# A QKV projection on one core: three leading row pairs multiplied without sums in place of two, and an identity tile of another size

## The chip, the cores and the metric

The kernel runs on one core of a Trainium2 chip. Its time is device microseconds for one execution; the time of a kernel is the median of its runs.

## The reference

```python
def reference(x, w_qkv):                      # x (16, 512, 768), w_qkv (768, 2304), float32
    qkv = np.matmul(x, w_qkv)
    hidden = x.shape[-1]
    q = qkv[..., :hidden]
    k = qkv[..., hidden:2*hidden]
    v = qkv[..., 2*hidden:]
    return np.stack([q, k, v], axis=0).astype(np.float32)
```

One product of 8192 rows by 768 by 2304, whose columns are written to three outputs. Both inputs are standard normal numbers.

## The kernel before

The 8192 rows are taken in 32 pairs of row blocks, 128 rows each. The 2304 columns are two "quads" of 1024 columns (q = 0 at the left, q = 1 at the right), each of two halves of 512, and a middle remainder of 256 columns. The 768 contraction rows are six slices of 128 (KT = 6), in two halves of three (KH = 3). So for a pair and a quad the product is one of 2 by 2 block matrices, and it is computed in one of two ways.

*Unsummed* (`block`, L378): plain bf16 matmuls, eight block products, that is 24 matmuls of 128x512 for a pair and a quad, 48 for a pair. `b1[q]` holds the bf16 weights of a quad's first column half, `bt` those of the second.

*Summed* (`do` and `product`, L193 to L246): seven products in place of eight, by Winograd's form of Strassen's method. Sums of x's blocks (`sums_x`, L177, on GpSimd) and of the weights' blocks (`sum_w`, L98, on VectorE) are multiplied, and the results are added up in PSUM and in the output tile. A pair costs 42 matmuls of 128x512. Products 1 and 2 use bf16 (`xb` and `b1`); the other five use f32r (float32r, 4 bytes an element): the stationary side is a slice of `s`, the moving side one of the four weight sums `t1` to `t4` or `b22`. The sums for quad 0 lie in `t_0`, in the w pool; those for quad 1 in two tiles `t_1`, which take over the buffers of the staged weights in pool tq.

In both ways the remainder is 12 bf16 matmuls of 128x256 for a pair (`rem`, L262).

Matmuls need x with its contraction axis on the partitions. For most pairs `load_x` brings x in 32-row groups with four DMAs, `transpose` (L124) turns 32x32 blocks on VectorE, and `round_x` (L175) casts to bf16 on GpSimd. The first three pairs are loaded as plain rows (`load_rows`) and turned by TensorE against an identity: pairs 0 and 1 after a cast to bf16 (`cast_rows`, `turn_bf16`, L158), pair 2 in fp32 (`turn_fp32`, L169), since its sums need fp32. `copy_two` (L139, L140) splits each of the casts and copies between VectorE and ScalarE.

The order of all work is written out by hand; each engine takes its instructions in the order of the program. At the start: warm-up matmuls on zeros, pairs 0 and 1 turned, block (0,0) [quad 0, first half] of pairs 0 and 1, their remainders, pair 2 turned, then blocks (0,1), (1,0) and (1,1) of pairs 0 and 1, with ScalarE casting the weights of the block that follows. Meanwhile VectorE makes the weight sums and GpSimd casts `bt0`'s second half (L376), `b22[0]` (L429) and `b22[1]` (L439) and makes pair 2's `xb` and sums. Pairs 2 to 31 are summed: `two` interleaves quad 0 (a) and quad 1 (b) of a pair in the order a1 b1 a2 a6 b2 b6 a5 a7 b5 b7 a4 remainder b4 a3 b3. Its `early`, after b1, transposes and sums the next pair and starts the load of the one after. The last pair has its own order (`last`).

SP issues nearly all DMAs, in order: three row loads and all the weights at the start, then stores and the loads of x. Of the output tiles `o` (two row blocks by 1024 columns) there are five buffers, of `xin` three, of `xb` four, of `xf` and `s` two. [...]

The w pool holds, in order of allocation, w_rem, b1 (2), b22 (2), t_0, zero, tiny and the identities; the pools that follow it in memory (tq, bt, o, st, xin, xf, xb, s) start where it ends.

Of the kernel before, what the change touches and what calls it, by code (L numbers as in the profile page):

```python
# [10 lines left out]
def kernel(  # L11
# [20 lines left out]
    nc = tc.nc  # L32
    P = 128
# [5 lines left out]
    KT = K // P  # L39
    KH = KT // 2  # L40
    KC = K // 4
    NP = M // (2 * P)
    CB = 512
# [3 lines left out]
    fp32 = mybir.dt.float32  # L47
# [51 lines left out]
    def sum_w(q, n):  # L99
        t1, t2, t3, t4 = ts[q]  # L100
        o, in0, in1 = {
            1: (t1, stage[q, 0, 1], stage[q, 0, 0]),
            2: (t2, stage[q, 1, 1], t1),
            3: (t3, stage[q, 1, 1], stage[q, 0, 1]),
            4: (t4, stage[q, 1, 0], t2),
        }[n]
        nc.vector.tensor_tensor(o, in0, in1, op=sub)
# [5 lines left out]
    def load_x(p, other):  # L113
        xin[p] = xin_pool.tile([P, 2 * P // G, KC], fp32, name="xin")
        t = xin[p]
        rows = x_flat[p * 2 * P:(p + 1) * 2 * P, :].rearrange("(g b) k -> b g k", b=G)
        for n in range(2):
            for h in range(2):
                i = 2 * h + n
                (nc.sync, other)[h].dma_start(t[i * G:(i + 1) * G], rows[:, :, i * KC:(i + 1) * KC])  # L120
# [13 lines left out]
        rows = x_flat[p * 2 * P:(p + 1) * 2 * P, :]  # L134
        nc.sync.dma_start(xin[p][:], rows.rearrange("(r m) k -> m r k", m=P))

    def copy_two(dst, src):

        nc.vector.tensor_copy(out=dst[0], in_=src[0])  # L139
        nc.scalar.activation(dst[1], src[1], ident)  # L140

    xc = {}

    def cast_rows(p):
        src = xin.pop(p)
        xc[p] = s_pool.tile([P, 2, K], bf16, name="xc", tag="s")
        for r in range(2):
            halves = (slice(0, K // 2), slice(K // 2, K))
            copy_two([xc[p][:, r, n] for n in halves], [src[:, r, n] for n in halves])

    def turn_bf16(p):
        c = xc.pop(p)
        xb[p] = xb_pool.tile([P, KT, 2 * P], bf16, name="xb")
        for r in range(2):
            cols = c[:, r, :].rearrange("m (p j) -> m j p", j=KT)
            ps = ps_pool.tile([P, KT, P], bf16, name="ps")
            for j in range(KT):
                nc.tensor.transpose(ps[:, j, :], cols[:, j, :], eye_b[:])  # L158
            ks = (slice(0, KH), slice(KH, KT))
            copy_two([xb[p][:, n, r * P:(r + 1) * P] for n in ks], [ps[:, n, :] for n in ks])  # L160

    def turn_fp32(p):
        src = xin.pop(p)
        xf[p] = xf_pool.tile([P, KT, 2 * P], fp32, name="xf")
        for r in range(2):
            cols = src[:, r, :].rearrange("m (p j) -> m j p", j=KT)
            ps = [ps_pool.tile([P, KH, P], fp32, name="ps") for _ in range(2)]
            for j in range(KT):
                nc.tensor.transpose(ps[j // KH][:, j % KH, :], cols[:, j, :], eye[:])  # L169
            ks = (slice(0, KH), slice(KH, KT))  # L170
            copy_two([xf[p][:, n, r * P:(r + 1) * P] for n in ks], [t[:] for t in ps])

    def round_x(p):
        xb[p] = xb_pool.tile([P, KT, 2 * P], bf16, name="xb")
        nc.gpsimd.tensor_copy(out=xb[p][:], in_=xf[p][:])  # L175

    def sums_x(p):  # L177
        t = xf.pop(p)
        a11, a12 = t[:, :KH, :P], t[:, KH:, :P]
        a21, a22 = t[:, :KH, P:], t[:, KH:, P:]  # L180
        s = s_pool.tile([P, 5, KH, P], f32r, name="s")
        g = nc.gpsimd
        g.tensor_tensor(s[:, 1], a21, a22, op=add)  # L183
        g.tensor_tensor(s[:, 2], s[:, 1], a11, op=sub)  # L184
        g.tensor_tensor(s[:, 3], a11, a21, op=sub)  # L185
        g.tensor_copy(out=s[:, 0], in_=a22)
        g.tensor_tensor(s[:, 4], a12, s[:, 2], op=sub)  # L187
        sr[p] = s
# [5 lines left out]
    def quad(p, q):  # L194
        u = Quad()
        u.p, u.q = p, q
        u.o = o_pool.tile([P, 2, 2 * CB], fp32, name="o", tag="o")
        u.x = u.y = u.z = None
        return u
# [17 lines left out]
    def bank():  # L217
        return ps_pool.tile([P, CB], fp32, name="ps")
# [32 lines left out]
    def store_quad(u):  # L251
        if u.q == 0:
            nc.sync.dma_start(rows_of(0, u.p, 0, H), u.o[:, :, :H])
            nc.sync.dma_start(rows_of(1, u.p, 0, 2 * CB - H), u.o[:, :, H:])
        else:
            part = 2 * H - Q_OFF[1]
            nc.sync.dma_start(rows_of(1, u.p, H - part, H), u.o[:, :, :part])
            nc.sync.dma_start(rows_of(2, u.p, 0, H), u.o[:, :, part:])
# [8 lines left out]
    def rem(p):  # L267
        ps = ps_pool.tile([P, 2, REM], fp32, name="ps")
        for r in range(2):
            rem_row(p, r, ps[:, r, :])  # L270
        o = or_pool.tile([P, 2, REM], fp32, name="orem")
        nc.scalar.activation(o[:], ps[:], ident)  # L272
        nc.sync.dma_start(rows_of(1, p, R_OFF - H, R_OFF - H + REM), o[:])
# [67 lines left out]
        rem_stored(1)  # L341


    zero = w_pool.tile([P, CB], bf16, name="zero")
    nc.vector.memset(zero[:], 0.0)
    load_rows(0)
    tiny = w_pool.tile([P, 1], fp32, name="tiny")
    nc.scalar.activation(tiny[:], zero[:, :1], ident)
    eye = w_pool.tile([P, P], fp32, name="eye")
    make_identity(nc, eye)  # L350
    eye_b = w_pool.tile([P, P], bf16, name="eye_b")
    make_identity(nc, eye_b)
    load_rows(1)
    load_blocks(0, 0, 1)
    st_rem = o_pool.tile([P, KT, REM], fp32, name="str", tag="o")
    load_w(st_rem[:], 0, KT, R_OFF, REM)
    load_rows(2)
    load_blocks(0, 1)
    o0 = [quad(p, 0) for p in range(2)]
    load_blocks(1, 0)  # L360
    load_blocks(1, 1)
    o1 = [quad(p, 1) for p in range(2)]

    def busy(n):

        ps = bank()
        for _ in range(n):
            nc.tensor.matmul(ps[:], zero[:, :P], zero[:], start=True, stop=True)

    def cast(q, h, c, w, eng):  # L370

        dst = w[:, h * KH:(h + 1) * KH, :]
        if eng is nc.scalar:
            eng.activation(dst, stage[q, h, c], ident)  # L374
        else:
            eng.tensor_copy(out=dst, in_=stage[q, h, c])  # L376

    def block(q, c, w, groups, cast_next):  # L378


        ps = [bank() for _ in range(4)]
        for js, tiles in groups:
            for n in tiles:
                p, r = divmod(n, 2)
                for j in js:
                    nc.tensor.matmul(  # L386
                        ps[n][:], xb[p][:, j, r * P:(r + 1) * P], w[:, j, :],
                        start=(j == 0), stop=(j == KT - 1), skip_group_check=True,
                    )
                if KT - 1 not in js:  # L390
                    continue
                if r == 0:
                    cast_next(p)
                o = (o0, o1)[q][p]
                nc.scalar.activation(o.o[:, r, c * CB:(c + 1) * CB], ps[n][:], ident)
                if c == 1 and r == 1:
                    store_quad(o)

    halves = [(range(h * KH, (h + 1) * KH), range(4)) for h in range(2)]
    singles = [((0, ), (0, 1)), ((1, ), (0, 1)), ((0, 1), (2, 3))]
    singles += [((j, ), range(4)) for j in range(2, KT)]

# [1 line left out]
    def cast_k(j):  # L406
        dve.tensor_copy(out=b1[0][:, j, :], in_=stage[0, j // KH, 0][:, j % KH, :])

    busy(11)
    cast_rows(0)  # L410
    turn_bf16(0)
    busy(4)
    cast_rows(1)
    cast_k(0)
    cast_k(1)
    turn_bf16(1)
    for j in range(2, KT):
        cast_k(j)
    act.activation(w_rem[:, KH:], st_rem[:, KH:], ident)
# [1 line left out]
    bt0 = bt_pool.tile([P, KT, CB], bf16, name="bt")  # L421
    bt1 = bt_pool.tile([P, KT, CB], bf16, name="bt")

    def cast_next(q, c, w):

        return lambda h: cast(q, h, c, w, act)

    cast(0, 1, 1, bt0, nc.gpsimd)
    nc.gpsimd.tensor_copy(out=b22[0][:], in_=stage[0, 1, 1])  # L429
    block(0, 0, b1[0], singles, lambda h: None)  # L430
    rem(0)
    rem(1)
    turn_fp32(2)
    cast(0, 0, 1, bt0, act)
    round_x(2)
    sums_x(2)
    for n in range(1, 5):
        sum_w(0, n)
    nc.gpsimd.tensor_copy(out=b22[1][:], in_=stage[1, 1, 1])  # L439
    block(0, 1, bt0, halves, cast_next(1, 0, b1[1]))  # L440
    load_x(3, nc.sync)
    block(1, 0, b1[1], halves, cast_next(1, 1, bt1))
    block(1, 1, bt1, halves, lambda h: None)
    t_1 = [tq_pool.tile([P, 2, KH, CB], f32r, name=f"t_1{n}", tag="tq") for n in range(2)]
    ts[1] = [t_1[n // 2][:, n % 2] for n in range(4)]
    for n in range(1, 5):
        sum_w(1, n)

    for p in range(2, NP):
        def early():  # L450
            if p + 1 < NP:
                transpose(p + 1)
                round_x(p + 1)
                sums_x(p + 1)
            if p + 2 < NP:
                load_x(p + 2, nc.scalar)

        if p < NP - 1:
            two(quad(p, 0), quad(p, 1), early)
        else:  # L460
            last(quad(p, 0), quad(p, 1))
# [30 lines left out]
```

## Time and profile before

| | us |
|---|---|
| median of 8 runs | 368.46 |
| lowest and highest | 368.23, 369.96 |
| the profiled execution's own time | 369.96 |
| its span, first to last instruction | 368.2 |
| TensorE busy | 360.0 |
| VectorE busy | 229.5 |
| GpSimd busy | 191.7 |
| ScalarE busy | 185.5 |

The profile is of one execution. PE is TensorE's matmuls, PEld its weight loads, which overlap them, DVE is VectorE, ACT is ScalarE, POOL is GpSimd, SP the engine that issues DMAs. L212 is line 212 of the kernel before. A row of groups has the line, the engine, the operation, what it writes and reads with shapes, how many there are, busy us, mean ns of one, and the idle time in front with what ended it. Matmuls are pipelined and their ends are modelled, so a matmul's price is the spacing of starts and not its own duration.

DMA moved 108.09 MB, 294 GB/s over the span, and the mean granted clock of TensorE was 0.993 of full speed.

### The profile page before, as it was taken

How to read it: one execution, taken by the hardware profiler on the slowest of the kernel's cores; microseconds unless marked ns; L12 is line 12 of the kernel's file. 1: busy time of each engine (PE TensorE's matmuls, PEld its weight loads, DVE VectorE, ACT ScalarE, POOL GpSimd, SP SyncE). 2: the span in 40 equal slices, each digit the busy share in tenths (PEclk: the TensorE clock that was granted, in tenths of full speed). 3: DMA queues.
4: the chain of work that ended last, by engine and by line, in shares of the span. 5: the costliest groups of instructions: out<-in, count | busy, mean ns of one | idle time of the engine just before them, and what ended most of it. 6: DMA issues, size and time to landing. Idle time of an engine off the chain costs nothing.

```text
span 368.2 us, 5286 instructions
## 1 busy us (share of the span) xinstructions
PE 360.0 (98%) x1791; PEld 246.9 (67%) x1791; DVE 229.5 (62%) x235; ACT 185.5 (50%) x307; POOL 191.7 (52%) x191
## 2 busy tenths in 40 slices
PE   7979999999999999999999999999999999999995
PEld 3634666677767677766667776766776666777673
DVE  3399766555666655576655566665557665556632
ACT  4557645454444454544545444445454454544442
POOL 1089944466544456644456654445664444665420
PEclk9989999999999999999999999999999999999998
DMA  7999888889988889998888998988899888999767
GB/s 297 380 386 337 275 268 284 291 281 300 318 281 274 283 293 280 314 305 272 280 293 275 305 317 266 293 280 296 276 314 308 272 279 291 283 299 317 266 232 281
DMA packets 80618, 108.09 MB, mean 294 GB/s; under 512 B 4816, under 2 KB 60368, under 8 KB 80592
## 3 DMA queue, kind: packets, MB, share of 16 engines
q1 hardware_dynamic: 64640, 95.96, 79.6%
q10 hardware_dynamic: 15952, 11.80, 10.0%
q8 instruction: 14, 0.23, 0.3%
q14 instruction: 12, 0.10, 0.1%
HBM read 32.24 MB, written 75.50 MB: 293 GB/s over the span
## 4 chain that ended last, share of the span: by engine, by line
PE 96%; DMA 1%; ACT 1%; DVE 0%; issue 0%
PE ps L212 78%; PE ps L262 12%; PE ps L386 6%; DMA xin<-in_x_dram 1%; PE ps L169 0%; PE ps L158 0%; ACT bt L374 0%; ACT xc L140 0%; ACT xb L140 0%; ACT xf L140 0%; ACT orem L317 0%; DVE xb L139 0%
## 5 line engine op out<-in xcount | busy, mean ns | idle before, releaser
L212 PE MATMUL ps<-t,s 128*128 128x512 f32 x720 | 194.5, 412 | 0.0
L212 PEld LDWEIGHTS ps<-t,s 128*128 128x128 f32 x720 | 133.2, 188 | 32.0
L175 POOL CAST xb<-xf 128x1536 bf16<-128x1536 f32 x30 | 45.4, 1515 | 139.5 <-DVE xf L124 139.5
L212 PE MATMUL ps<-b,xb 128*128 128x512 bf16 x360 | 88.1, 381 | 0.0
L124 DVE STREAM_TRANSPOSE xf<-xin 128x1536 f32<-128x1536 f32 x29 | 87.0, 3000 | 0.1
L246 DVE TENSOR_TENSOR o<-o,ps 128x512 f32<-128x512 f32 x60 | 41.3, 688 | 62.4 <-PE ps L212 62.3
L240 DVE TENSOR_TENSOR o<-o,ps 128x512 f32<-128x512 f32 x60 | 41.3, 688 | 58.4 <-ACT o L239 58.4
L212 PEld LDWEIGHTS <-xb 128*128 128x128 bf16 x360 | 30.5, 98 | 44.5 <-issue 16.0
L239 ACT ACTIVATE o<-ps 128x512 f32<-128x512 f32 x60 | 36.0, 600 | 46.8 <-PE ps L212 46.8
L226 ACT ACTIVATE o<-ps 128x512 f32<-128x512 f32 x60 | 35.9, 599 | 45.2 <-DVE o L246 40.6
L233 ACT ACTIVATE o<-ps 128x512 f32<-128x512 f32 x60 | 36.0, 599 | 43.4 <-PE ps L212 43.4
L262 PE MATMUL ps<-w_rem,xb 128*128 128x256 bf16 x384 | 47.5, 273 | 0.0
L212 PE MATMUL ps<-b,s 128*128 128x512 f32 x180 | 46.5, 393 | 0.0
L262 PEld LDWEIGHTS <-xb 128*128 128x128 bf16 x384 | 35.0, 98 | 12.4 <-issue 8.4
L212 PEld LDWEIGHTS ps<-b,s 128*128 128x128 f32 x180 | 33.8, 188 | 8.0
L230 DVE TENSOR_TENSOR o<-o,ps 128x512 f32<-128x512 f32 x60 | 37.9, 677 | 2.0 <-ACT o L226 1.3
L243 ACT ACTIVATE o<-ps 128x512 f32<-128x512 f32 x60 | 35.9, 598 | 4.8 <-ACT orem L317 0.4
L184 POOL TENSOR_TENSOR s<-s,xf 128x384 fp32r<-128x384 f32 x30 | 31.9, 1064 | 2.4
L187 POOL TENSOR_TENSOR s<-xf,s 128x384 fp32r<-128x384 f32 x30 | 32.0, 1066 | 0.0
L183 POOL TENSOR_TENSOR s<-xf 128x384 fp32r<-128x384 f32 x30 | 31.9, 1064 | 0.0
L185 POOL TENSOR_TENSOR s<-xf 128x384 fp32r<-128x384 f32 x30 | 31.6, 1053 | 0.0
L272 ACT ACTIVATE orem<-ps 128x512 f32<-128x512 f32 x31 | 18.6, 600 | 22.7 <-PE ps L262 22.7
(40 smaller groups left out, 122.8 us busy)
## 6 DMA issues: line engine op xcount, KB each, us to landing
out_dram<-o SPq DMA_DIRECT2D x62, 768.0 KB, 4.9
out_dram<-o SPq DMA_DIRECT2D x65, 256.0 KB, 4.6
xin<-in_x_dram SPq DMA_DIRECT2D x60, 192.0 KB, 6.7
xin<-in_x_dram ACTq DMA_DIRECT2D x56, 192.0 KB, 5.5
out_dram<-orem SPq DMA_DIRECT2D x31, 256.0 KB, 2.4
st<-in_w_qkv_dram SPq DMA_DIRECT2D x6, 768.0 KB, 14.2
xin<-in_x_dram SPq DMA_DIRECT2D x3, 768.0 KB, 5.8
st<-in_w_qkv_dram SPq DMA_DIRECT2D x6, 256.0 KB, 6.2
```

Source lines behind the costliest of these rows:

```text
L124: nc.vector.transpose(t[:].rearrange("p j (g b) -> p g j b", b=G), xin.pop(p)[:].rearrange("p g (a j) -> p g j a", a=G),)
L175: nc.gpsimd.tensor_copy(out=xb[p][:], in_=xf[p][:])
L187: g.tensor_tensor(s[:, 4], a12, s[:, 2], op=sub)
L212: nc.tensor.matmul(ps[:], lhs[j], rhs[j], start=(start and j == 0), stop=(j == KH - 1), skip_group_check=True,)
L226: nc.scalar.activation(c11, u.x[:], ident)
L230: nc.vector.tensor_tensor(c11, c11, u.z[:], op=add)
L233: nc.scalar.activation(c12, u.x[:], ident)
L239: nc.scalar.activation(c22, u.x[:], ident)
L240: nc.vector.tensor_tensor(c22, c22, u.y[:], op=add)
L243: nc.scalar.activation(c21, u.x[:], ident)
L246: nc.vector.tensor_tensor(c12, c12, u.y[:], op=add)
L262: nc.tensor.matmul(ps, xb[p][:, j, r * P:(r + 1) * P], w_rem[:, j, :], start=(j == 0), stop=(j == KT - 1), skip_group_check=True,)
```

## The change

Three pairs (NS = 3) are multiplied unsummed, and pair 3 is the first that is summed. Pair 2 is cast to bf16 and turned like pairs 0 and 1, but VectorE alone does its casts and copies. After the remainders of pairs 0 and 1 and the turning of pair 2 comes block (0,0) of pair 2 by itself; the other blocks run over six row blocks in place of four. GpSimd's casts of bt0 and b22 and ScalarE's cast of bt0's first half go to VectorE. `load_x(3)` is issued with the loads of the start, `load_x(4)` takes the old place of `load_x(3)`. Pair 3's transpose, cast and sums stand between quad 1's weight sums. The two identity tiles (128 fp32 and 128 bf16 elements) become one of 240 bf16 elements, of which 128 are used.

```diff
-    def copy_two(dst, src):
+    def copy_halves(dst, src, two):
         nc.vector.tensor_copy(out=dst[0], in_=src[0])
-        nc.scalar.activation(dst[1], src[1], ident)
+        if two:
+            nc.scalar.activation(dst[1], src[1], ident)
+        else:
+            nc.vector.tensor_copy(out=dst[1], in_=src[1])
...
-    def turn_fp32(p):
...
+    NS = 3
...
-    eye = w_pool.tile([P, P], fp32, name="eye")
+    eye = w_pool.tile([P, 240], bf16, name="eye")[:, :P]
     make_identity(nc, eye)
-    eye_b = w_pool.tile([P, P], bf16, name="eye_b")
-    make_identity(nc, eye_b)
     load_rows(1)
...
-    o0 = [quad(p, 0) for p in range(2)]
     load_blocks(1, 0)
     load_blocks(1, 1)
-    o1 = [quad(p, 1) for p in range(2)]
+    load_x(3, nc.sync)
+    quads = [[quad(p, q) for p in range(NS)] for q in range(2)]
...
-    cast(0, 1, 1, bt0, nc.gpsimd)
-    nc.gpsimd.tensor_copy(out=b22[0][:], in_=stage[0, 1, 1])
-    block(0, 0, b1[0], singles, lambda h: None)
+    block(0, 0, b1[0], singles, nothing)
     rem(0)
     rem(1)
-    turn_fp32(2)
-    cast(0, 0, 1, bt0, act)
-    round_x(2)
-    sums_x(2)
+    cast_rows(2, False)
+    turn_rows(2, False)
+    block(0, 0, b1[0], halves((4, 5)), nothing)
+    for h in range(2):
+        cast(0, h, 1, bt0, dve)
     for n in range(1, 5):
         sum_w(0, n)
-    nc.gpsimd.tensor_copy(out=b22[1][:], in_=stage[1, 1, 1])
-    block(0, 1, bt0, halves, cast_next(1, 0, b1[1]))
-    load_x(3, nc.sync)
-    block(1, 0, b1[1], halves, cast_next(1, 1, bt1))
-    block(1, 1, bt1, halves, lambda h: None)
+    dve.tensor_copy(out=b22[0][:], in_=stage[0, 1, 1])
+    block(0, 1, bt0, halves(range(6)), cast_next(1, 0, b1[1]))
+    load_x(4, nc.sync)
+    block(1, 0, b1[1], halves(range(6)), cast_next(1, 1, bt1))
+    block(1, 1, bt1, halves(range(6)), nothing)
+    rem(2)
     t_1 = [tq_pool.tile([P, 2, KH, CB], f32r, name=f"t_1{n}", tag="tq") for n in range(2)]
     ts[1] = [t_1[n // 2][:, n % 2] for n in range(4)]
-    for n in range(1, 5):
-        sum_w(1, n)
-
-    for p in range(2, NP):
+    sum_w(1, 1)
+    sum_w(1, 2)
+    transpose(3)
+    round_x(3)
+    sums_x(3)
+    sum_w(1, 3)
+    sum_w(1, 4)
+    dve.tensor_copy(out=b22[1][:], in_=stage[1, 1, 1])
+
+    for p in range(NS, NP):
```

More of the change, by code (lines that the diff above doesn't have):

```diff
@@ L135, in load_rows, with cast_rows @@
         nc.sync.dma_start(xin[p][:], rows.rearrange("(r m) k -> m r k", m=P))
-    def copy_two(dst, src):
+    def copy_halves(dst, src, two):
         nc.vector.tensor_copy(out=dst[0], in_=src[0])
-        nc.scalar.activation(dst[1], src[1], ident)
+        if two:
+            nc.scalar.activation(dst[1], src[1], ident)
+        else:
+            nc.vector.tensor_copy(out=dst[1], in_=src[1])
     xc = {}
-    def cast_rows(p):
+    def cast_rows(p, two=True):
         src = xin.pop(p)
@@ L148, in cast_rows, with turn_rows @@
             halves = (slice(0, K // 2), slice(K // 2, K))
-            copy_two([xc[p][:, r, n] for n in halves], [src[:, r, n] for n in halves])
-    def turn_bf16(p):
+            copy_halves([xc[p][:, r, n] for n in halves], [src[:, r, n] for n in halves], two)
+    def turn_rows(p, two=True):
         c = xc.pop(p)
@@ L157, in turn_bf16 @@
             for j in range(KT):
-                nc.tensor.transpose(ps[:, j, :], cols[:, j, :], eye_b[:])
+                nc.tensor.transpose(ps[:, j, :], cols[:, j, :], eye)
             ks = (slice(0, KH), slice(KH, KT))
-            copy_two([xb[p][:, n, r * P:(r + 1) * P] for n in ks], [ps[:, n, :] for n in ks])
-    def turn_fp32(p):
[L163 to L171, printed above, removed]
+            copy_halves(
+                [xb[p][:, n, r * P:(r + 1) * P] for n in ks], [ps[:, n, :] for n in ks], two
+            )
     def round_x(p):
@@ L378, in block @@
     def block(q, c, w, groups, cast_next):
-        ps = [bank() for _ in range(4)]
+        ps = {}
         for js, tiles in groups:
@@ L384, in block @@
                 p, r = divmod(n, 2)
+                if n not in ps:
+                    ps[n] = bank()
                 for j in js:
@@ L393, in block, with halves @@
                     cast_next(p)
-                o = (o0, o1)[q][p]
-                nc.scalar.activation(o.o[:, r, c * CB:(c + 1) * CB], ps[n][:], ident)
+                u = quads[q][p]
+                nc.scalar.activation(u.o[:, r, c * CB:(c + 1) * CB], ps[n][:], ident)
                 if c == 1 and r == 1:
-                    store_quad(o)
-    halves = [(range(h * KH, (h + 1) * KH), range(4)) for h in range(2)]
+                    store_quad(u)
+    def halves(tiles):
+        return [(range(h * KH, (h + 1) * KH), tiles) for h in range(2)]
     singles = [((0, ), (0, 1)), ((1, ), (0, 1)), ((0, 1), (2, 3))]
@@ L407, in cast_k, with cast_next @@
         dve.tensor_copy(out=b1[0][:, j, :], in_=stage[0, j // KH, 0][:, j % KH, :])
+    def cast_next(q, c, w):
+        return lambda p: p < 2 and cast(q, p, c, w, act)
+    def cast_k(j):
+        dve.tensor_copy(out=b1[0][:, j, :], in_=stage[0, j // KH, 0][:, j % KH, :])
+    nothing = lambda p: None
     busy(11)
     cast_rows(0)
-    turn_bf16(0)
+    turn_rows(0)
     busy(4)
@@ L415 @@
     cast_k(1)
-    turn_bf16(1)
+    turn_rows(1)
     for j in range(2, KT):
@@ L422 @@
     bt1 = bt_pool.tile([P, KT, CB], bf16, name="bt")
-    def cast_next(q, c, w):
-        return lambda h: cast(q, h, c, w, act)
-    cast(0, 1, 1, bt0, nc.gpsimd)
-    nc.gpsimd.tensor_copy(out=b22[0][:], in_=stage[0, 1, 1])
-    block(0, 0, b1[0], singles, lambda h: None)
+    block(0, 0, b1[0], singles, nothing)
     rem(0)
     rem(1)
-    turn_fp32(2)
-    cast(0, 0, 1, bt0, act)
-    round_x(2)
-    sums_x(2)
+    cast_rows(2, False)
[3 more added lines that the diff above has]
+        cast(0, h, 1, bt0, dve)
     for n in range(1, 5):
         sum_w(0, n)
-    nc.gpsimd.tensor_copy(out=b22[1][:], in_=stage[1, 1, 1])
-    block(0, 1, bt0, halves, cast_next(1, 0, b1[1]))
-    load_x(3, nc.sync)
-    block(1, 0, b1[1], halves, cast_next(1, 1, bt1))
-    block(1, 1, bt1, halves, lambda h: None)
+    dve.tensor_copy(out=b22[0][:], in_=stage[0, 1, 1])
[4 more added lines that the diff above has]
+    rem(2)
     t_1 = [tq_pool.tile([P, 2, KH, CB], f32r, name=f"t_1{n}", tag="tq") for n in range(2)]
     ts[1] = [t_1[n // 2][:, n % 2] for n in range(4)]
-    for n in range(1, 5):
-        sum_w(1, n)
-    for p in range(2, NP):
+    sum_w(1, 1)
[7 more added lines that the diff above has]
+    for p in range(NS, NP):
         def early():
```

## The prediction

> **What bounds the kernel now.** I read the busy shares first, then the chain of work that ended last, then stretches of time, then groups by form. The page gives the first two:
>
> ```profile
> PE 360.0 (98%) x1791; PEld 246.9 (67%) x1791; DVE 229.5 (62%) x235; ACT 185.5 (50%) x307; POOL 191.7 (52%) x191
> ...
> PE 96%; DMA 1%; ACT 1%; DVE 0%; issue 0%
> ```
>
> TensorE is busy nearly all the time and the chain hardly leaves it. So only two things can shorten the span: taking TensorE's few gaps out of the start, and making each matmul shorter. The chain in order of time (start, length, what) shows both:
>
> ```profile
> 14.08 2.70 PE ps L262 x24
> 16.78 1.62 PE ps L169 x12
> 18.40 0.02 issue
> 18.43 0.49 ACT xf L140
> 18.92 1.38 ACT bt L374
> 20.30 0.04 issue
> 20.34 17.39 PE ps L386 x72
> 37.73 7.47 PE ps L212 x33
> 45.20 1.33 PE ps L262 x12
> 46.53 9.54 PE ps L212 x42
> ```
>
> After the remainders (L262) and pair 2's fp32 turning (L169), TensorE waits until 20.34 for ScalarE to cast bt0 (L374), because ScalarE first had to copy the turned fp32 columns (L140). From 37.73 on the summed pairs run: 42 product matmuls in 9.54 us and 12 of the remainder in 1.33 us, so 10.87 us each, thirty times. Stretches (us, busy PE, PEld, DVE, ACT, POOL, clock, DMA share, GB/s):
>
> ```profile
> 16.78:18.39 1.61, 1.61 (x12) 1.44 (x12) 0.92 (x2) 1.09 (x2) 0.00 (x0) 1.00 1.05 387
> 18.39:20.34 1.95, 0.00 (x0) 0.00 (x0) 1.92 (x3) 1.86 (x2) 0.93 (x1) 1.00 1.05 387
> 20.34:27.20 6.86, 6.86 (x24) 2.74 (x24) 6.86 (x3) 3.17 (x4) 6.86 (x3) 0.75 1.05 385
> 27.20:32.38 5.18, 5.18 (x25) 2.35 (x24) 5.15 (x3) 4.92 (x7) 5.10 (x4) 1.00 1.05 404
> ```
>
> The third and fourth rows hold the same work, 24 bf16 matmuls of one block. At clock 1.00 they take 5.18 us, 215.8 ns each; right after the idle 1.95 us the clock is 0.75 and they take 6.86. The stall thus costs twice, 1.95 and then 1.68 us. Now the forms:
>
> ```profile
> L212 PE MATMUL ps<-t,s 128*128 128x512 f32 x720 | 194.5, 412 | 0.0
> L212 PEld LDWEIGHTS ps<-t,s 128*128 128x128 f32 x720 | 133.2, 188 | 32.0
> L212 PEld LDWEIGHTS <-xb 128*128 128x128 bf16 x360 | 30.5, 98 | 44.5 <-issue 16.0
> L107 DVE TENSOR_TENSOR t<-st,st x3: 1748/2547/2550, 18.5 to 33.9; 128x1536 fp32r<-128x1536 f32 x3
> L107 DVE TENSOR_TENSOR t<-st x1: 3009/3009/3009, 23.1 to 23.1; 128x1536 fp32r<-128x1536 f32 x1
> ```
>
> A matmul's own duration overlaps its neighbour, so I price by spacing. Of a pair's 42 products 12 are bf16 (products 1 and 2): 12 x 215.8 ns = 2.59 us. The other 30 are f32r (float32r, 4 bytes) and take 9.54 - 2.59 = 6.95 us, 231.7 ns each, 15.9 ns more than bf16. They are not all alike: from 184.56 to 185.69 us five start in 1.13 us, 226.6 ns each, while the slowest steps reach 238 ns, and the pattern comes back in every pair. It is no random interference, then; something fixed, such as addresses, may matter.
>
> **What the Trainium skill says.** "TensorE: Matmul & The Clock Gate", Part 1, says that the clock halves when TensorE lacks matmul work for a window of some 3.4 us. The trace agrees in kind: 1.61 us of transposes plus 1.95 us idle come before the 0.75 clock. The same page, section on weight-path perf modes, says that the fast weight load serves 16-bit weights and not FP32; 98 against 188 ns above agrees. "SBUF - State Buffer", Specifications and Operand start alignment, knows 16-byte lines and a start rule of one element, and says that it timed nothing there; a shift by 32 bytes would then be free. The trace neither confirms nor refutes this. The same page, Who interferes with whom, says that a VectorE instruction with two SBUF inputs contends with GpSimd reading SBUF. It agrees: the sum beginning at 18.50, mostly alone, took 1.75 us, and 3.01 us beside GpSimd casts.
>
> **The change, part by part.** (a) Pair 2 no longer needs the fp32 turning, so bt0's casts leave ScalarE and GpSimd for VectorE and TensorE does 12 matmuls of block (0,0) meanwhile. This fills the 1.95 us. VectorE should be done with pair 2's copies near 18.7 and with both bt0 halves near 20.9 (2 x 1.1 us, an estimate: twice the 0.56 us of the 128x768 cast), and block (0,1) wants the first half near 20.5. The second half's data landed at 19.4 in the trace. Gain 1.95.
> (b) Without idle time the slow clock should not come: gain 1.68; if it comes, nothing.
> (c) Twelve bf16 transposes replace twelve fp32 ones: the earlier dozen ran from 5.62 to 6.40, 0.78 against 1.61 us. Gain 0.83.
> (d) A new wait: TensorE needs VectorE's copy of each row block before block (0,0) goes on. All four casts and four copies (0.36 and 0.35 us) are now VectorE's. The casts hide under the 2.70 us of remainders; the first copy (0.35) and its signal do not. Cost 0.4, at most 0.9. Queued behind it on TensorE is everything.
> (e) Pair 2 costs 48 x 215.8 ns + 1.33 = 11.69 us in place of 10.87. Cost 0.82.
> (f) VectorE also takes b22's two casts and issues the first summed pair's transpose between sums. GpSimd, rid of its start-up casts, leaves VectorE's first four sums alone. From 20.9: four sums at 1.75 (27.9), b22[0] 1.1 (29.0), two sums (32.5), transpose 3.0 (35.5). GpSimd then casts and forms s[1], s[2] at contended prices, 2.98 + 2.49 + 2.39: 43.4. TensorE starts pair 3 at 16.78 + 0.78 + 0.4 + 120 x 0.2158 + 1.33 = 45.2 and wants s[2] after nine matmuls, at 47.1. Hidden, with 3.7 us to spare; without that cover it is the slower rival below.
> (g) Moved queues: load_x(3) goes up SP's queue ahead of the remainder stores, load_x(4) goes behind three pairs' stores. Up to seven output tiles contend for five buffers; the first reused store leaves about 27.5 and its buffer is wanted about 35. Stores took 4.9 us in the median. Cost 0, at most 1.
> Sum (a) to (g): -1.95 - 1.68 - 0.83 + 0.4 + 0.82 = -3.2 us.
> (h) The identity tile. Before, eye and eye_b take 512 + 256 bytes; after, one tile takes 480, so everything allocated after the w pool moves down 288 bytes. In the built programs x's sums, xb, t_1 and bt began 32 bytes past a multiple of 64, and now begin on one; b1, b22 and t_0 already did. All now share one place in 512 bytes. The trace has no f32r matmul with such weights, so this is bounded from both sides: at best the bf16 spacing, 15.9 ns less on 29 pairs x 30 = 870 matmuls, 13.8 us; at worst all at 238 ns, 870 x 6.3 = 5.5 us more. I take the fastest spacing seen in this trace, 226.6: 870 x 5.1 ns = 4.4 us. A bf16 matmul with xb at the same 32 bytes loses nothing, which warns against more; f32r loads 188 ns of weights per matmul, which leaves less slack.
>
> Total -7.6. The profiled execution took 369.96 us, 1.76 around its span of 368.2; it becomes 362.4. It lies 1.5 above the median of 368.46, from which the same difference gives 360.8.
>
> **Rivals.** *Addresses do nothing*: 368.46 - 3.2 = 365.2. For it: line size by the skill, and t_1 against t_0 shows no clear order. Against: the fixed pattern. *Addresses do everything*: f32r at 215.8, 351.4. For it: an f32r weight load of 188 ns plus the 40 ns seen between its end and the next start makes about the whole spacing, so a slightly shorter load would reach the streaming time. Against: no f32r matmul here went under 226. DMA would follow: a pair moves about 3.1 MB, in 10.4 us 302 GB/s, against 404 seen. *Slower*: the VectorE chain of (f). If all sums cost 3.0 us although GpSimd is idle, six of them add 7.5 us, s[2] comes at 50.9, TensorE stalls 3.8 us in front of pair 3 and pays the slow clock's 1.7 again: 365.2 + 5.5 = 370.7 with addresses doing nothing. It decides from about 2.4 us a sum for a stall, and about 2.6 for a loss. Against it: the 1.75 us measured. *The change does not do what it says*, the stall surviving at another place: about 368.
>
> **Chances.** Forecast (f32r about 222 to 229 ns) 0.34; addresses nothing 0.27; everything, or nearly, 0.24; slower 0.10; the surviving stall and mixtures 0.05. The range 350.8 to 366.5 takes in the first three with their spread and leaves out about 0.17. A measurement of this kernel can tell 0.3%, 1.1 us, from no change. Faster is the sum of the first three and part of the last, 0.87; same 0.03; slower 0.10.
>
> **What would show it.** (a), (b): no TensorE gap over 0.6 us between 16.8 and 45, clock 1.00 from 20 on. (e), (f): L212 begins near 45.2, against 48.5 for pair 3 before. (h): the chain's rows of 42 products at 9.39 us (forecast), 9.54 (nothing) or 9.06 (everything), and the f32 weight load at or under 188 ns. The prediction is wrong if those rows lengthen, or if a gap appears in front of the first summed pair.

## The result and the profile after

The kernel after takes 365.04 us (median of 11 runs, 364.92 to 365.72), the kernel before, measured with it, 368.51 us (32 runs): a ratio of 0.990, 95% interval 0.9887 to 0.9913. That is 3.47 us less, clear of the 1.1 us that the prediction took for noise, where 7.6 us were forecast. The profiled execution took 365.72 us, its span is 363.6.

One thing is needed to read these numbers: 24 of these 32 runs of the kernel before lie at 368.1 to 368.7 us, the other 8 at 369.8 to 370.5, and the one that was profiled, at 369.96, is one of the 8.

The page of the kernel after:

```profile
PE 357.2 (98%) x1797; PEld 244.7 (67%) x1797; DVE 226.2 (62%) x239; ACT 182.3 (50%) x304; POOL 173.5 (48%) x180
...
PE 97%; ACT 1%; ACTq 0%; DVE 0%; issue 0%
```

TensorE bounds it as before. The chain in order of time (start, length, what), where L382 is `block`, L256 the remainder, L161 the turning and L206 `product`:

```profile
9.62 5.18 PE ps L382 x24
14.80 2.62 PE ps L256 x24
17.42 0.35 PE ps L161 x6
17.77 0.02 issue
17.79 0.37 DVE xb L139
18.16 0.05 issue
18.21 26.07 PE ps L382 x120
44.28 1.31 PE ps L256 x12
45.59 7.40 PE ps L206 x33
53.00 1.33 PE ps L256 x12
54.32 9.48 PE ps L206 x42
```

The stall of 1.95 us is gone; in its place stands a wait of 0.44 us for VectorE's first copy of pair 2, and then 120 unsummed matmuls run without a break. The row of 42 products is 9.48 us long, against 9.54 before and 9.39 in the forecast. The same in stretches (us; busy PE, PEld, DVE, ACT, POOL; clock; DMA share; GB/s), where the clock stays at 1.00 through the unsummed blocks:

```profile
17.42:18.21 0.79, 0.67 (x14) 0.53 (x11) 0.42 (x2) 0.60 (x1) 0.00 (x0) 1.00 1.03 381
18.21:20.81 2.60, 2.60 (x12) 1.19 (x13) 2.60 (x6) 0.45 (x1) 0.00 (x0) 1.00 1.05 386
20.81:28.58 7.77, 7.77 (x37) 3.53 (x36) 7.74 (x6) 5.22 (x8) 0.00 (x0) 1.00 1.07 345
```

And the forms. The weight loads of f32r are as long as before, 188 ns. VectorE's sums have come down from some 2.6 us in the median to 1.75; GpSimd is idle beside the first six of them, and the one at 37.31, beside GpSimd's own work on pair 3, took 3.02:

```profile
L206 PEld LDWEIGHTS ps<-t,s 128*128 128x128 f32 x696 | 128.8, 188 | 29.6
L107 DVE TENSOR_TENSOR t<-st,st x3: 1716/1751/1754, 20.6 to 35.7; 128x1536 fp32r<-128x1536 f32 x3
L107 DVE TENSOR_TENSOR t<-st x1: 1752/1752/1752, 24.1 to 24.1; 128x1536 fp32r<-128x1536 f32 x1
```

Between the two profiled executions the span fell by 4.6 us. From the first block to the first summed pair that both have in common, pair 3, it is 48.46 - 8.90 = 39.56 us before and 45.43 - 9.62 = 35.81 after, 3.75 less. A pair takes 10.807 us in place of 10.873, 0.067 less, 1.9 us over 29 pairs. Two things go the other way. The turning of pair 0 took from 5.85 to 7.12 us in this execution (0.78 us long before), and the first block began 0.7 us later; that is not the median's, 0.68 us lower: all_shifted_32 (below), profiled at 365.01 us with the same schedule, began its first block 0.72 us earlier. And from the start of the last matmul to the end of the span it is 4.85 us in place of 4.48.

### The profile page after: what moved, and what is told of

It reads as the page before. It is cut to its first block, busy times and chain, and to the rows that moved or that the text cites. A ratio compares the mean times of both kernels' runs of the same rounds, so it can differ in the third digit from the quotient of the medians.

```text
span 363.6 us, 5274 instructions
## 1 busy us (share of the span) xinstructions
PE 357.2 (98%) x1797; PEld 244.7 (67%) x1797; DVE 226.2 (62%) x239; ACT 182.3 (50%) x304; POOL 173.5 (48%) x180
## 4 chain that ended last, share of the span: by engine, by line
PE 97%; ACT 1%; ACTq 0%; DVE 0%; issue 0%
PE ps L206 75%; PE ps L256 11%; PE ps L382 9%; PE ps L362 1%; PE ps L161 1%; ACT o L237 0%; ACTq L297 0%; ACT orem L311 0%; DVE xb L139 0%; ACT xb L141 0%; ACT xc L141 0%; ACTq L313 0%; DVE zero L340 0%; ACTq L311 0%
## 5 line engine op out<-in xcount | busy, mean ns | idle before, releaser
L206 PE MATMUL ps<-t,s 128*128 128x512 f32 x696 | 186.5, 410 | 0.0
L206 PEld LDWEIGHTS ps<-t,s 128*128 128x128 f32 x696 | 128.8, 188 | 29.6
L169 POOL CAST xb<-xf 128x1536 bf16<-128x1536 f32 x29 | 43.9, 1513 | 170.6 <-DVE xf L124 170.6
L206 PE MATMUL ps<-b,xb 128*128 128x512 bf16 x348 | 85.2, 381 | 0.0
L240 DVE TENSOR_TENSOR o<-o,ps 128x512 f32<-128x512 f32 x58 | 39.7, 688 | 59.0 <-PE ps L206 59.0
L234 DVE TENSOR_TENSOR o<-o,ps 128x512 f32<-128x512 f32 x58 | 39.8, 688 | 51.4 <-ACT o L233 51.4
L206 PEld LDWEIGHTS <-xb 128*128 128x128 bf16 x348 | 29.4, 98 | 42.7 <-issue 14.5
L233 ACT ACTIVATE o<-ps 128x512 f32<-128x512 f32 x58 | 34.7, 598 | 44.1 <-PE ps L206 44.1
L220 ACT ACTIVATE o<-ps 128x512 f32<-128x512 f32 x58 | 34.7, 597 | 42.7 <-DVE o L240 34.1
L227 ACT ACTIVATE o<-ps 128x512 f32<-128x512 f32 x58 | 34.8, 600 | 42.1 <-PE ps L206 42.1
L256 PE MATMUL ps<-w_rem,xb 128*128 128x256 bf16 x384 | 47.5, 273 | 0.0
L206 PE MATMUL ps<-b,s 128*128 128x512 f32 x174 | 44.5, 391 | 0.0
L256 PEld LDWEIGHTS <-xb 128*128 128x128 bf16 x384 | 35.2, 98 | 11.9 <-issue 7.8
L224 DVE TENSOR_TENSOR o<-o,ps 128x512 f32<-128x512 f32 x58 | 36.5, 667 | 3.1 <-ACT o L220 1.8
L206 PEld LDWEIGHTS ps<-b,s 128*128 128x128 f32 x174 | 32.7, 188 | 7.5
L237 ACT ACTIVATE o<-ps 128x512 f32<-128x512 f32 x58 | 34.7, 599 | 4.2 <-ACT orem L311 0.4
L178 POOL TENSOR_TENSOR s<-s,xf 128x384 fp32r<-128x384 f32 x29 | 30.0, 1035 | 2.3
L177 POOL TENSOR_TENSOR s<-xf 128x384 fp32r<-128x384 f32 x29 | 30.9, 1064 | 0.0
L181 POOL TENSOR_TENSOR s<-xf,s 128x384 fp32r<-128x384 f32 x29 | 29.6, 1020 | 0.0
L179 POOL TENSOR_TENSOR s<-xf 128x384 fp32r<-128x384 f32 x29 | 29.1, 1004 | 0.0
```

The lines of the kernel that those rows point to most:

```text
L206: nc.tensor.matmul(ps[:], lhs[j], rhs[j], start=(start and j == 0), stop=(j == KH - 1), skip_group_check=True,)
L220: nc.scalar.activation(c11, u.x[:], ident)
L224: nc.vector.tensor_tensor(c11, c11, u.z[:], op=add)
L227: nc.scalar.activation(c12, u.x[:], ident)
L233: nc.scalar.activation(c22, u.x[:], ident)
L234: nc.vector.tensor_tensor(c22, c22, u.y[:], op=add)
```

## The experiments

**Schedule and addresses taken apart.** Two kernels do half of the change each.

The schedule alone:

```diff
-    eye = w_pool.tile([P, 240], bf16, name="eye")[:, :P]
+    eye = w_pool.tile([P, P], bf16, name="eye")
```

> The kernel after with an identity tile of 128 elements in place of 240: the schedule of the change, without its shift of addresses (all tiles behind the w pool start 32 bytes past a multiple of 64 again). Theory A, the addresses set the f32r spacing: pairs of 10.87 us as in the kernel before, rows of 42 products at 9.54 us, time about 365.0 + 1.9 = 366.9 us. Rival B, the shorter pairs of the kernel after come from the order or phase of the work and not from addresses: pairs stay at 10.81 us, time 365.0 us.

Measured: 367.05 us, ratio to the kernel before 0.996 (0.9949 to 0.9973); 10.873 us a pair.

The addresses alone, on the kernel before:

```diff
...
-    eye = w_pool.tile([P, P], fp32, name="eye")
+    eye = xf_pool.tile([P, P], fp32, name="eye", tag="xf")
...
-    eye_b = w_pool.tile([P, P], bf16, name="eye_b")
+    eye_b = w_pool.tile([P, 240], bf16, name="eye_b")[:, :P]
```

> The kernel before with the same addresses behind the w pool as the kernel after: the fp32 identity lies in a buffer of the xf pool and the bf16 one has 240 elements. Schedule as before. Theory A: pairs of 10.81 us, thirty of them save 2.0 us, about 366.5 us. Rival B: pairs of 10.87 us, time 368.5 us.

Measured: 366.28 us, ratio 0.994 (0.9916 to 0.9958); 10.807 us a pair.

So the addresses, as theory A has it, are worth 2.0 us, in either schedule (368.25 - 366.28 and 367.05 - 365.04; 368.25 is the kernel before measured beside these two), and 29 or 30 pairs at 0.067 us are just that. The schedule is worth only 1.2 us in the medians (368.25 - 367.05 and 366.28 - 365.04), where the prediction had 3.2.

TensorE itself gains more by the schedule. From the start of the first block to the start of the last row of the remainder it is 8.70 to 359.32 us with the addresses alone and 9.46 to 358.17 in the kernel after, 1.9 us less. Of this 0.3 is lost at the end, where the span runs on for 5.4 us in place of 5.1, and 0.35 outside the span: the device time is 2.1 to 2.2 us longer than the span in every run of the kernel after, and 1.7 to 1.9 in every run of the kernel before. Neither loss was forecast, and no run shows what makes them.

**The slow clock after the stall.** The edit, in the kernel before; the matmuls' result is used nowhere:

```diff
     turn_fp32(2)
+    busy(8)
```

> The kernel before with eight matmuls on zeros (no result is used) put behind pair 2's fp32 turning, so that TensorE is not idle while ScalarE casts bt0. Theory C: the slow clock after the stall comes only in some executions, those near 369.9 us (the profiled one among them), so filling the wait takes away that upper group and leaves the median at 368.3 to 368.5 us. Rival D: the slow clock comes in every execution, as the prediction's step (b) had it, so the median falls by 1.7 us to about 366.8 us.

Measured: 368.37 us, ratio 0.999 (0.998 to 1.0007), 14 runs from 368.16 to 368.91. Of 47 other runs of the kernel before, the eleven with 369.8 to 370.5 us had mean clocks of 0.992 to 0.995, the other 36 had 368.1 to 368.8 us and 0.997 to 1.000. With the wait filled none of 14 is in an upper group, nor is any of the 115 runs of the kernels here with the new schedule, which has no such wait: none of them lies more than 0.9 us above the fastest of its kernel. This is theory C. What it means can be seen in the profile of the kernel with the addresses alone, which has the same stall and happens to be an execution without the slow clock (stall, then the 24 matmuls behind it):

```profile
18.32:20.25 1.93, 0.00 (x0) 0.00 (x0) 1.90 (x3) 1.86 (x2) 0.91 (x1) 1.00 1.06 392
20.25:25.50 5.25, 5.20 (x24) 2.41 (x25) 5.25 (x2) 2.69 (x4) 5.25 (x3) 1.00 1.05 386
```

In the kernel before the same 24 matmuls took 6.86 us at a clock of 0.75; here they take 5.25 at 1.00. Both profiles have the stall; the slow clock comes behind it in about a quarter of the executions, if the eleven above are those that have it, as their mean clocks and the 1.6 us say.

**Which matmuls became faster.** TensorE alone in the kernel after (us; busy; clock; DMA share; GB/s): the last f32r matmul of a6 with the bf16 matmul behind it, the last two of b6 behind the next change from bf16, and the fourteen f32r matmuls that follow (a5 to a4):

```profile
112.68:113.15 0.47, 0.47 (x4) 1.00 0.97 359
113.81:114.27 0.46, 0.46 (x3) 1.00 0.89 183
114.27:117.45 3.18, 3.18 (x16) 1.00 1.06 348
```

The counts take in neighbours that reach into a stretch; by their starts the first row is 239 and 227 ns, the second two matmuls of 231.5 ns on average, and the third fourteen of 226.7 ns. In the kernel before no more than five in a row were that fast. So the forecast's fastest spacing is right for the long row and is not reached shortly behind a change. The order of products was therefore changed, in the kernel after (all of `two`):

```diff
-        do(a, 6)
         do(b, 2)
+        rem(a.p)
+        do(a, 6)
         do(b, 6)
...
         do(a, 4)
-        rem(a.p)
-        do(b, 4)
         do(a, 3)
         store_quad(a)
+        do(b, 4)
         do(b, 3)
```

> The kernel after with the products of a pair in another order: the twelve bf16 products and the remainder first (a1 b1 a2 b2 remainder), then all thirty f32r ones in a row (a6 b6 a5 a7 b5 b7 a4 a3 b4 b3). Theory E: the f32r matmuls that stay above 226.7 ns in the kernel after are those close behind a change from bf16 to f32r, and each change back costs about 11 ns; with one change a pair in place of three the pair falls from 10.81 to about 10.73 us, in all 2.0 us, time about 363.0 us. Rival F: the slow ones are slow by their operands (t2, t4, b22), whatever stands in front, so the pair stays at about 10.8 us and the time at 365.0 us; if a product then waits for an eviction, more.

Measured: 363.34 us, ratio to the kernel before 0.986 (0.9831 to 0.9883), so it beats both kernels; 10.760 us a pair. In its profile, the same view of nine f32r matmuls, from the second behind the change on, and then of eighteen:

```profile
102.77:104.85 2.08, 2.08 (x10) 1.00 1.08 396
104.85:108.93 4.08, 4.08 (x19) 1.00 1.06 272
```

That is 231 ns for each of nine, then 226.7 for each of eighteen. a3 and b4, slow in the kernel after, are now in the fast part, and a5, fast there, is in the slow part. So it is not the operand, as rival F had it, but the position behind the change. The gain is 1.7 us and not the 2.0 of theory E. Only 1.3 of it are the pairs, 28 times 0.047 us, since the slow part has grown to ten; the other 0.4 lies outside the span, where this kernel has 1.8 us in every run and the kernel after 2.1 to 2.2, for no reason that a run shows.

The same order with the addresses of the kernel before (the identity tile at 128 elements):

> The kernel with one change from bf16 to f32r a pair, but with an identity tile of 128 elements, so the addresses of the kernel before. If the f32r matmuls settle at 226.7 ns only with aligned operands, nothing settles in the long row either: about 231 to 232 ns throughout and the pair 10.85 us (two changes less at about 11 ns each), time about 366.4 us. If the long row settles whatever the addresses: 10.76 us a pair and 363.4 us, as with the padded tile.

Measured: 367.32 us, ratio 0.996 (0.9943 to 0.9971); 10.887 us a pair, where 10.85 was expected. The thirty f32r matmuls of a pair in its chain, which take 6.84 us in the kernel with the padded tile:

```profile
103.67 6.97 PE ps L206 x30
```

That is 232 ns each. Nothing settles, which was the point; but the time is no better than that of the old order with these addresses (367.05), so the step of 11 ns at a change is not a cost that can simply be saved. This part of theory E is wrong.

**Whose addresses, and which.** Six kernels move tiles in the kernel after. Each edit is one line or two:

In s_only_off, 32 bytes stand in front of the s pool:

```diff
+    pad_pool = ctx.enter_context(tc.tile_pool(name="pad", bufs=1))
     s_pool = ctx.enter_context(tc.tile_pool(name="s", bufs=2))
...
+    pad_pool.tile([P, 16], bf16, name="pad")
```

In t1_only_off the same pad stands behind the tq pool, and the identity tile gives the 32 bytes back:

```diff
-    eye = w_pool.tile([P, 240], bf16, name="eye")[:, :P]
+    eye = w_pool.tile([P, 224], bf16, name="eye")[:, :P]
```

The same line with 144 elements is all_64_bytes, with 176 apart_128 and with 368 apart_256. In all_shifted_32 the pad is the first tile of the w pool, in front of w_rem:

```diff
+    w_pool.tile([P, 16], bf16, name="pad")
```

> The kernel after with a 32-byte pad in front of the s pool: the stationary f32r operand starts 32 bytes past a multiple of 64 again, everything else stays where the kernel after has it. Theory G, the stationary side's start counts: pairs back near 10.87 us, time about 366.9 us. Rival H, only the moving side t_1 counts: 10.81 us, 365.0 us. Rival I, what counts is that the moving and the stationary tile sit at one place in 64 bytes (in the kernel before only t_1 and s did, and the fastest stretch lay in products with t_1): now neither t_0 nor t_1 agrees with s, so slower than the kernel before has it, pairs of 10.9 us or more, about 367.5 us.

> The kernel after with quad 1's weight sums t_1 (and the staging buffers that they take over) 32 bytes lower, at 32 past a multiple of 64; a pad brings all that follows back to where the kernel after has it. Theory G, the stationary side counts: pairs stay at 10.81 us, 365.0 us. Rival H, the moving side counts: near 10.87 us, about 366.9 us. Rival I, agreement counts: quad 0's products stay fast and quad 1's fall back, about half, 10.84 us and 366.0 us.

> The kernel after with an identity tile of 144 elements in place of 240: all tiles behind the w pool still start at a multiple of 64 bytes, but 192 bytes lower, so that they no longer share their place in 128 or 512 bytes with t_0, b1 and b22. If a multiple of 64 is enough: 365.0 us, pairs of 10.81 us. If the tiles have to share one place in 128 or 512 bytes: near 366.9 us, pairs of 10.87 us.

> The kernel after with a 32-byte pad in front of the w pool: every operand, t_0, b22, t_1 and s alike, now starts 32 bytes past a multiple of 64, and all still share one place in 512 bytes. If the moving and the stationary f32r tile have to sit at the same place (theory I), nothing is lost: pairs of 10.81 us, 365.0 us. If they have to start at a multiple of 64 or 128 themselves: pairs of 10.87 to 10.93 us, 367 to 368.6 us.

> The kernel after with an identity tile of 176 elements: s and t_1 at a multiple of 512 bytes, t_0 and b22 at 128 past one, all at a multiple of 128. If sharing a place in 128 bytes is enough: 365.0 us. If it has to be 256 or 512 bytes: slow like the tiles 192 bytes apart, 10.87 to 10.92 us a pair and 367 to 368.3 us.

> The kernel after with an identity tile of 368 elements: s and t_1 at 384 past a multiple of 512 bytes, t_0 and b22 at 128 past one, so 256 bytes apart. If sharing a place in 128 or 256 bytes is enough: 365.0 us, pairs of 10.81 us. If it has to be 512 bytes: 367 to 368.3 us.

Measured, with the two kernels above that bear on it. The third and fourth columns say how far the stationary tile s lies from the moving tile, in bytes, whole multiples of 256 left out (the nearer way round); this follows from the sizes of the tiles in their order of allocation.

| kernel | start of s in 64 bytes | s from t_0, b22 | s from t_1 | us a pair | time, us | ratio to before |
|---|---|---|---|---|---|---|
| after | 0 | 0 | 0 | 10.807 | 365.04 | 0.9887 to 0.9913 |
| all_shifted_32 | 32 | 0 | 0 | 10.807 | 365.04 | 0.9892 to 0.9923 |
| apart_256 | 0 | 0 | 0 | 10.807 | 365.25 | 0.9894 to 0.9926 |
| schedule_only | 32 | 32 | 0 | 10.873 | 367.05 | 0.9949 to 0.9973 |
| t1_only_off | 0 | 0 | 32 | 10.893 | 367.47 | 0.9962 to 0.9984 |
| all_64_bytes | 0 | 64 | 0 | 10.920 | 368.26 | 0.9979 to 0.9998 |
| s_only_off | 32 | 32 | 32 | 10.927 | 368.64 | 0.9983 to 1.0008 |
| apart_128 | 0 | 128 | 0 | 10.940 | 368.61 | 0.999 to 1.0012 |

It is neither side's own alignment: with every tile 32 bytes past a multiple of 64 nothing is lost, and with every tile on a multiple of 64, or of 128, 3 us and more can be lost. What the three fast kernels share, and no other of the table has, is that the stationary and all moving f32r tiles sit at the same place in 256 bytes. Theory G falls by t1_only_off, which moves t_1 alone and lost 2.4 us, and rival H by s_only_off, which moves s alone and lost 3.6. Of the distances tried 256 is as good as 0, and 32, 64 and 128 are not; no other was tried.

Theory I, agreement, has the direction right throughout but not each size: for t1_only_off it gave 10.84 us and 366.0, and the measured 10.893 and 367.47 lie even above rival H's figures. The trace of t1_only_off shows what is right in it. TensorE alone, from the second matmul of a5 to the end of a7 (quad 0, which agrees), then b5 and b7 (quad 1, which does not):

```profile
114.33:115.47 1.14, 1.14 (x7) 1.00 1.05 320
115.47:116.87 1.40, 1.40 (x7) 1.00 1.11 384
```

By their starts the five of quad 0 are 226.8 ns each and the six of quad 1 233.7. In the kernel before, where t_1 agrees and t_0 does not, it is the other way round: the six of a5 and a7 are 232.3 each, and the five fast ones lie in b5 and b7. But agreement of its own tiles is not enough for a product. In t1_only_off a4 and a3, which agree, follow quad 1's slow products and stay at 229 to 237 ns, so more is lost than theory I had counted; and in apart_128 b5 and b7 never settle (224 to 238 ns), although t_1 agrees there.

The chain of apart_128, one remainder and the products of one pair (one matmul's record is missing where "issue" stands, so the products take 2.10 + 0.07 + 7.44 = 9.61 us):

```profile
106.96 1.33 PE ps L256 x12
108.28 2.10 PE ps L206 x9
110.39 0.07 issue
110.46 7.44 PE ps L206 x32
```

The same of apart_256, where the products take 2.07 + 0.07 + 7.34 = 9.48 us:

```profile
106.83 1.33 PE ps L256 x12
108.15 2.07 PE ps L206 x9
110.23 0.07 issue
110.30 7.34 PE ps L206 x32
```

The remainder, bf16, is the same to the last digit; the products differ by 0.13 us. The recorded f32r weight load is 188 to 189 ns in every one of these kernels, so the loss is not seen there. Why the place in 256 bytes counts, why a distance of 64 or 128 costs more than one of 32, and why a row needs three to ten matmuls to settle, no run explains.

## Why the prediction was wrong, point by point

- *What bounds it, and that f32r spacing hangs on something fixed*: right. "It is no random interference, then; something fixed, such as addresses, may matter" is what the runs found.
- *(a) the stall filled, 1.95*: right; between 16.8 and 45 us no gap over 0.44 us remains.
- *(b) the slow clock, 1.68*: right for the execution that was profiled and wrong for the median, the number that was forecast. The first step that failed is "from which the same difference gives 360.8". The profiled execution lay 1.5 us above the median because it had the slow clock, which most executions do not have. Its 1.68 us was already missing from the 368.46 from which it was subtracted. The term is 0 in the median, as the filled wait shows: 368.37 against 368.25.
- *(c), (d) turning and the new wait*: the turning with its wait ends 0.79 us after the remainders, where 0.78 + 0.4 was allowed: the second six transposes run while TensorE would wait anyway. 0.4 us better.
- *(e) pair 2 unsummed, 0.82*: as sized; 120 matmuls in 26.07 us are 217 ns each.
- *(f) VectorE's longer queue*: right, with the first six sums at 1.75 us. GpSimd had s[2] ready at 42.86, and the products began at 45.4. The slower rival's point of decision, 2.4 us a sum, was not neared.
- *(g) moved queues*: nothing on the chain up to the last matmul. The 0.3 us at the end and the 0.35 outside the span, a loss of the schedule, are terms that the prediction did not have; whether the queues have a part in them is open.
- *(h) the addresses, 4.4*: right sign, and the second step that failed: sized more than twice too big, 2.0 us. The forecast let all thirty f32r matmuls of a pair reach 226.6 ns, but only those further behind a change from bf16 do. The 5.1 ns a matmul should have been 2.2 (0.067 us over 30). Of the two descriptions that it gave of the new addresses, a start on a multiple of 64 is not what counts (all_shifted_32), sharing one place is. That a shift by 32 bytes would be free, as its reading of 16-byte lines had it, is true of all tiles together (all_shifted_32) and false of one against another: moving t_1 alone by 32 bytes cost 2.4 us.

In sum: (a) to (g) without (b) were forecast as 1.6; TensorE gained 1.9, since (c) and (d) went better, and 0.65 was lost at the end and outside the span, which leaves the 1.2 of schedule_only. With 2.0 for (h) that is 3.2 (368.25 - 365.04); 368.51 as the time before gives 3.47. Against the 7.6 forecast, 1.7 are missing by (b) and 2.4 by (h). The rival "addresses do nothing" gave 365.2, next to the result, and is wrong all the same: without the addresses' share the time is 367.05. It came near because it counted the 1.68 of (b) that the median never had.

## What to carry to other kernels

Before a profiled execution's stages are priced, its own time is to be held against the median: if it lies off, the stage that makes the difference must be found and left out, or it is saved twice. Where matmuls stream without slack, look at the spacing of starts position by position: a pattern that repeats exactly is a matter of layout and order, and one padded tile may be worth as much as a new schedule. With f32r, try the stationary and the moving tiles at one place in 256 bytes, and then the f32r products in one row; without the first the second gained nothing here.

## What the runs showed of the hardware that was not expected

- f32r matmuls of 128x512 settle at a spacing of 226.7 ns. Where tiles do not agree, the thirty of a pair take 232 ns each in the mean before the change and up to 234 in apart_128 (9.61 us less twelve bf16 at 215.8 ns). bf16 has 215.8 at every address tried.
- The distance of stationary and moving f32r tile in 256 bytes moved a pair of 10.807 us by up to 0.133 (128 apart), and the start in 64 bytes did not move it at all.
- After a change from bf16 the fast spacing sets in only after three to ten f32r matmuls whose tiles agree (three at b6 in the kernel after, ten in one_switch).
- A wait of 1.95 us behind 1.61 us of fp32 transposes went with 1.6 us more and a lower mean clock in 11 of 47 executions; in the one of this kind that was traced, the next 24 matmuls took 6.86 us at a clock of 0.75 in place of 5.25.
